# Attention's output projection by halves of the tokens, with the second tile's squares added on VectorE

## The chip, the cores and the metric

The kernel runs on one core of one Trainium2 chip. The metric is the device time of one execution in microseconds. Before the change it is 2884.4 us, the median of three runs (2883.95 to 2885.89).

## The reference

A trunk of two layers over 1040 tokens (1024 tokens with 16 meta tokens ahead of them), 1024 columns wide, all in float32. The first layer is a state-space mixer with a gated feed-forward network, the second a stick-breaking attention (16 heads of 64) with another such network. What the change touches is the end of the attention and the start of the last network:

```python
def _rmsnorm(x, g):
    x32 = x.astype(jnp.float32)
    y = x32 * lax.rsqrt(jnp.mean(x32 * x32, axis=-1, keepdims=True) + NORM_EPS)
    return (y * g.astype(jnp.float32)).astype(x.dtype)

def _conv_ffn(u, w_up, conv_w, conv_b, w_down):
    h = _causal_dwconv(u @ w_up, conv_w, conv_b)
    g, val = jnp.split(h, 2, axis=-1)
    return (jax.nn.silu(g) * val) @ w_down

    # in reference(), for each layer
            o = _stick_breaking_attention(q, k_shared, v_shared).reshape(b, L, SB_WIDTH)
            h = h + o @ sb_w_o[j]
        h = h + _conv_ffn(_rmsnorm(h, ffn_norm[layer]), ffn_w_up[layer], ffn_conv_w[layer],
                          ffn_conv_b[layer], ffn_w_down[layer])
    return _rmsnorm(h, final_norm)[:, N_META:]
```

The outputs of the meta tokens are dropped, so the second layer's network is computed for the 1024 others and for the two tokens ahead of them that its convolution needs.

## The kernel before

**Layout and precision.** The stream `h` is held with columns on partitions: eight rows of 128 columns, each a buffer with all tokens along it. The last stage works on four tiles of 256 tokens (the first 258 wide, with the two lead tokens), in two halves of two tiles. TensorE multiplies float32 as three products of rounded parts (`mm3`): high weight by high operand (L195), high by low (L196), low by high (L197). "A product" below is one such instruction. Before TensorE can use them, weights and operands are split:

- Weights go through `load_w`: SyncE issues the DMA (L176) into one of three buffers, ScalarE copies the high part (L182), and Pool subtracts it to make the low part (L99), in pieces of 256 columns. High and low parts have three buffers each.
- Halves of an attention row go through `split_half`: ScalarE copies (L213), VectorE subtracts (L214). Whole rows go through `split`, in thirds (L205, L206).
- Rows of `h`, operands and some weights share a pool of 28 row buffers.

**The output projection.** The attention leaves its result `o` in memory as eight pairs of heads, 128 columns each. `o_proj` first fetches and splits pairs 0 to 3 as whole rows and the first halves of pairs 4 and 5, while pairs 6 and 7 are still being computed by the attention. Then come the *blocks*: for each of the eight output rows one block of weights (`w_o_f[f]`, 768 columns for six pairs) and the four tiles, six pairs for the tiles of the first half and four for those of the second. Then `enter_ffn` runs the *tiles*: for each tile in turn all eight output rows with the pairs that were left, which are 6 and 7 for the tiles 0 and 1, and 4 to 7 for the tiles 2 and 3.

Each sum over pairs is collected in a PSUM bank, an *accumulator*, and VectorE adds it to `h` (`accumulate`, L520). The blocks take their banks from two pools with three banks together, the tiles from three pools with five.

**What follows each tile.** Its squares (ScalarE, `square_row`) are summed over partitions and rows on TensorE by a product with a matrix of ones: for tile 0 VectorE adds the eight rows' squares up first (L1045) and one such product follows (L1023); for the tiles 1 to 3 each row has its own (L1049). From the sums `factors` makes the norm's factors (ScalarE L975 to L977, VectorE L979 to L981). `forms` then makes what the up projection of a half multiplies: the normed rows (sixteen instructions on VectorE, L1071, called the products of the forms), differences of them (L1095), and high and low parts (ScalarE L1077, VectorE L1078). `store` writes the tile's rows of `h` to memory (L1010, in SyncE's queue). `up_weights` fetches and splits the up projection's weights (Pool, L99); `up` multiplies, and VectorE adds partial results in PSUM (L1217) before further products go on into the same bank.

**What sets the order.** The program is written engine by engine in the order of the code; around this place a scheduler places instructions of each engine by a simulated timeline, while the attention itself keeps the order that is written. Within an engine instructions run in that order, and SyncE issues the DMAs one by one.

## Time and profile before

| what | value |
| --- | --- |
| median of three runs | 2884.4 us |
| the profiled execution | 2880.28 us |
| its span | 2878.6 us |
| TensorE busy | 2826.2 us, 98% of the span |
| VectorE busy | 2093.7 us, 73% |
| ScalarE busy | 1630.2 us, 57% |
| Pool busy | 1626.2 us, 56% |
| granted TensorE clock, mean | 0.998 |

The span is the time from the first to the last recorded instruction; the execution's own time is 1.7 us longer. The profile names the engines PE (TensorE), PEld (its weight loads), DVE (VectorE), ACT (ScalarE), POOL and SP (SyncE). A row of a timeline gives the start from the beginning of the span, the duration, the engine, the line of the kernel, the instruction, its output and inputs and their shapes, and how many instructions it stands for; behind it, in brackets, how long the engine was idle before it and what ended that. The output projection and the four tiles lie between 2070 and 2190 us of the span; the last network follows to the end.

### The profile page before, as it was taken

To read this page: it belongs to the slowest core of one execution; us is meant where nothing else is said; L and a number is where in the kernel's file an instruction comes from. 1 tells how busy PE (TensorE), PEld (TensorE's weight loads), DVE (VectorE), ACT (ScalarE), POOL (GpSimd) and SP (SyncE) were. 2 spreads that over 40 slices of the span, in tenths; PEclk is the share of its full clock that TensorE was granted. 3 is DMA by queue.
4 is the path that set the end of the run, shared out by engine and by line. 5 is a ranking of instruction groups with operands and counts; after the bars stand their busy time and mean duration, and the time that the engine had idled before them with its cause. 6 is when DMAs were issued, how large, how long until landed. Compare 5 with 4: busy or idle time off the path is not lost.

```text
span 2878.6 us, 58687 instructions
## 1 busy us (share of the span) xinstructions
PE 2826.2 (98%) x21859; PEld 2710.5 (94%) x21859; DVE 2093.7 (73%) x4068; ACT 1630.2 (57%) x3393; POOL 1626.2 (56%) x2440
## 2 busy tenths in 40 slices
PE   8999999999999999999999999999999999999998
PEld 7989999999989999999999999999898999999888
DVE  5676666668597767676886888888759776767776
ACT  5554454543265656555336888887736555555433
POOL 2366455643529888868853222222363888886882
PEclk9999999999999999999999999999999999999999
DMA  4333334333412222244132222222432222225331
GB/s 118 85 112 98 114 86 135 105 131 101 130 59 97 77 80 78 79 167 159 53 121 71 65 61 70 61 59 54 138 115 75 80 80 81 76 82 183 110 103 67
DMA packets 135578, 274.51 MB, mean 95 GB/s; under 512 B 15827, under 2 KB 68188, under 8 KB 135292
## 3 DMA queue, kind: packets, MB, share of 16 engines
q1 hardware_dynamic: 129484, 258.85, 28.8%
q0 software_dynamic: 2096, 6.77, 0.6%
q10 hardware_dynamic: 3712, 5.15, 0.5%
q8 instruction: 172, 2.82, 0.4%
q14 instruction: 114, 0.93, 0.1%
HBM read 204.63 MB, written 51.16 MB: 89 GB/s over the span
## 4 chain that ended last, share of the span: by engine, by line
PE 45%; DVE 2%; ACT 1%; POOL 1%; issue 1%; DMA 0%; ACTq 0%; DVEq 0%; SPq 0%; POOLq 0%
PE p L197 5%; PE p L195 5%; PE p L196 5%; PE acc L197 4%; PE acc L195 4%; PE acc L196 4%; PE pj L195 3%; PE pj L196 3%; PE pj L197 3%; PE po L1658 3%; PE lg L1617 3%; PE wT L1644 3%; POOL wl L99 1%; DVE h L1071 0%; ACT bt L1621 0%
## 5 line engine op out<-in xcount | busy, mean ns | idle before, releaser
L99 POOL TENSOR_TENSOR wl<-w,wh 128x256 fp32r<-128x256 f32 x768 | 685.7, 924 | 367.3 <-ACT wh L182 265.9
L195 PE MATMUL pj<-uh,wh 128*128 128x348 f32 (+2 forms) x1536 | 501.4, 327 | 3.9 <-DVE qs L1568 1.6
L196 PE MATMUL pj<-ul,wh 128*128 128x348 f32 (+2 forms) x1536 | 495.2, 322 | 0.1
L197 PE MATMUL pj<-uh,wl 128*128 128x348 f32 (+2 forms) x1536 | 492.1, 320 | 0.0
L195 PE MATMUL p<-bh,fh 128*128 128x262 f32 (+1 forms) x1408 | 400.6, 285 | 5.5 <-DVE p L1217 5.5
L197 PE MATMUL p<-bh,fl 128*128 128x262 f32 (+1 forms) x1408 | 400.7, 285 | 1.9 <-POOL fl L99 1.9
L196 PE MATMUL p<-bl,fh 128*128 128x262 f32 (+1 forms) x1408 | 397.8, 283 | 0.1
L99 POOL TENSOR_TENSOR fl<-x,fh 128x256 fp32r<-128x256 f32 x352 | 265.1, 786 | 191.6 <-ACT fh L1154 165.7
L195 PE MATMUL p<-bh,wh 128*128 128x262 f32 (+1 forms) x1040 | 295.0, 284 | 1.9 <-ACT ft L1214 1.9
L196 PE MATMUL p<-bl,wh 128*128 128x262 f32 (+1 forms) x1040 | 295.3, 284 | 1.4 <-DVE bl L1078 1.4
L195 PEld LDWEIGHTS pj<-uh,wh 128*128 128x128 f32 x1536 | 289.0, 188 | 7.5 <-issue 1.9
L197 PE MATMUL p<-bh,wl 128*128 128x262 f32 (+1 forms) x1040 | 294.2, 283 | 0.0
L196 PEld LDWEIGHTS pj<-ul,wh 128*128 128x128 f32 x1536 | 289.5, 188 | 1.5 <-DVE ul L306 0.4
L197 PEld LDWEIGHTS pj<-uh,wl 128*128 128x128 f32 x1536 | 289.0, 188 | 0.1
L325 DVE SCALAR_TENSOR_TENSOR c<-p,params,c 128x260 f32<-128x260 f32 (+1 forms) x528 | 248.5, 480 | 54.9 <-ACT c L322 48.4
L195 PEld LDWEIGHTS p<-bh,fh 128*128 128x128 f32 x1408 | 267.4, 190 | 6.3 <-DVE p L1217 5.9
L197 PEld LDWEIGHTS p<-bh,fl 128*128 128x128 f32 x1408 | 266.6, 189 | 2.9 <-POOL fl L99 2.5
L196 PEld LDWEIGHTS p<-bl,fh 128*128 128x128 f32 x1408 | 267.7, 190 | 0.5 <-DVE bl L1078 0.4
L1214 ACT ACTIVATE ft<-p 128x262 f32<-128x262 f32 (+1 forms) x352 | 133.1, 383 | 176.4 <-DVE p L1217 110.3
L197 PE MATMUL acc<-gh,wl 128*128 128x260 f32 (+1 forms) x672 | 213.9, 320 | 2.6 <-POOL wl L99 2.5
L196 PE MATMUL acc<-gl,wh 128*128 128x260 f32 (+1 forms) x672 | 214.1, 320 | 0.0
L195 PE MATMUL acc<-gh,wh 128*128 128x260 f32 (+1 forms) x672 | 211.0, 320 | 3.0 <-DVE h L1378 2.9
(344 smaller groups left out, 7918.3 us busy)
## 6 DMA issues: line engine op xcount, KB each, us to landing
w<-in_w_up SPq DMA_DIRECT2D x88, 512.0 KB
w<-in_w_down SPq DMA_DIRECT2D x44, 512.0 KB
w<-in_w_in SPq DMA_DIRECT2D x40, 512.0 KB
E<-ea_d SPq DMA_DIRECT2D x32, 464.0 KB
D<-acs_d SPq DMA_DIRECT2D x32, 420.5 KB
g<-c SPq DMA_DIRECT2D x88, 130.0 KB
g<-c SPq DMA_DIRECT2D x88, 128.0 KB
b<-g SPq DMA_DIRECT2D x16, 520.0 KB
```

The source lines that it names most:

```text
L99: eng.tensor_tensor(out[:, c], x[:, c], y[:, c], op=op)
L195: self.behind(mm(out, wh, uh, start=first, stop=False, skip_group_check=joins), tie, "behind the sums of squares")
L196: mm(out, wh, ul, start=False, stop=False, skip_group_check=joins)
L197: self.last_mm = mm(out, wl, uh, start=False, stop=last, skip_group_check=joins)
L325: ins = nc.vector.scalar_tensor_tensor(out, ps[:, o + i : o + i + n], wcol(i), out, op0=ALU.mult, op1=ALU.add)
L1214: nc.scalar.activation(s[:, :N], ps[:, :N], AF.Copy)
L1617: nc.tensor.matmul(ps[:nt, :m], part[:, c0 : c0 + nt], ks[a][:, s0 : s0 + m], start=x == 0, stop=x == 1)
L1644: nc.tensor.transpose(pt[:ns, x * CB : x * CB + nt], bt[a][:nt, x * CB : x * CB + ns], self.ident[:nt, :nt])
L1658: nc.tensor.matmul(po[64 * a : 64 * a + 64, :nt], v[: CH[c][1], c, 64 * a : 64 * a + 64], wt[a][: CH[c][1], c, :nt], start=x == 0, stop=x ...
```

## The change

In the second layer the work is put in another order, by halves of the tokens:

- **Blocks by halves.** First the eight rows' blocks for the tiles 0 and 1 (six pairs), then the tiles 0 and 1 with pairs 6 and 7, then the eight rows' blocks for the tiles 2 and 3 (pairs 0 to 3), then the tiles 2 and 3 with pairs 6, 7, 4 and 5. Each block's weights are fetched and split once for each half (768 columns, then 512 of them again).
- **Operands.** Every row of `o` is fetched and split as a half; the second half's operands are made behind the tiles of the first.
- **Forms.** The factors of tile 1 and the forms of the first half run beside the blocks of the second half; before, they ran beside the tiles 2 and 3.
- **Squares.** Tile 1's squares are added on VectorE, as tile 0's were, and one product with ones follows in place of eight.
- **Up weights.** The first block of up weights is split behind the blocks of the second half; before, ahead of the tiles.

The first layer calls the same function with a pair in place of the callable, and keeps its order.

```diff
--- before.py
+++ after.py
@@ -957,12 +957,12 @@
         def operands(x):
             made[x] = last[x][0], last[x][1]()
 
-        def tile(j, work):
+        def tile(j, work, m=1):
             ws, ops = made[j // 2]
             ms[j] = self.sm("ms")
             for f in range(KD):
                 self.accumulate(h, f, *g.span(j), lambda i, f: (ws[i][0][:, f * P : f * P + P], ws[i][1][:, f * P : f * P + P]), ops, HB, next(banks), g.part(j // 2)[0])
-                self.square_row(ms[j], h, f, *g.span(j), KD if j == 0 else 1)
+                self.square_row(ms[j], h, f, *g.span(j), m)
                 next(work, None)
 
         def factors(j):
@@ -1010,24 +1010,31 @@
                 nc.sync.dma_start(d[k, :, c : c + n], h[k][:, HB + c : HB + c + n])
 
         self.after_factors = None
-        ws0 = list(self.up_weights(layer, 0, pool))[-1]
+        split = callable(last[1])
+        if not split:
+            ws0 = list(self.up_weights(layer, 0, pool))[-1]
         operands(0)
-        tile(0, iter(()))
+        tile(0, iter(()), KD)
         store(0)
-        operands(1)
+        if not split:
+            operands(1)
         forms = [form_tiles()]
         work = self.forms(layer, h, r, 0, forms[0], pool)
 
-        def first(sums):
+        def first(j, sums, n):
             yield
-            nc.tensor.matmul(ms[0][:, : g.span(0)[1]], self.ones, sums, start=True, stop=True)
-            factors(0)
+            nc.tensor.matmul(ms[j][:, : g.span(j)[1]], self.ones, sums, start=True, stop=True)
+            factors(j)
             yield
-            yield from islice(work, 3)
-
-        tile(1, first(self.squares))
-        factors(1)
+            yield from islice(work, n)
+
+        tile(1, first(0, self.squares, 3), KD if split else 1)
         store(1)
+        if split:
+            made[1] = last[1](first(1, self.squares, KD))
+            ws0 = list(self.up_weights(layer, 0, pool))[-1]
+        else:
+            factors(1)
         for j in (2, 3):
             tile(j, work)
             factors(j)
@@ -1742,18 +1749,27 @@
             self.nc.sync.dma_start(t, od[p, :, g.at + s0 : g.at + s0 + m])
             return self.split_half(t, "o")
 
-        tiles = [(n // 3 * i, n // 3) for i in range(3)]
-        ops = [self.split(fetch(od[p], "o"), "o", tiles=tiles) for p in range(first - 2)]
-        ops = [ops + [part(p, 0) for p in (first - 2, first - 1)], ops]
-        for f in range(KD):
-            w = self.load_w(a["w_o_f"][f], first * P)
-            h[f] = fetch(hd[f], "h")
-            for j in range(4):
-                self.accumulate(h, f, *g.span(j), lambda i, f: (w[0][:, i * P : i * P + P], w[1][:, i * P : i * P + P]), ops[j // 2], HB, base=-g.lead)
+        def columns(x, count, ops, work):
+            for f in range(KD):
+                w = self.load_w(a["w_o_f"][f, :, : count * P], count * P)
+                if x == 0:
+                    h[f] = fetch(hd[f], "h")
+                for j in (2 * x, 2 * x + 1):
+                    self.accumulate(h, f, *g.span(j), lambda i, f: (w[0][:, i * P : i * P + P], w[1][:, i * P : i * P + P]), ops, HB, base=g.part(x)[0])
+                next(work, None)
+
+        columns(0, first, [part(p, 0) for p in range(first)], iter(()))
         ops = [part(p, 0) for p in range(first, PAIRS)]
-        ws = [self.load_wd(a["w_o"][first - 2 + i], i < 2) for i in range(4)]
-        second = [part(p, 1) for p in range(first - 2, PAIRS)]
-        return self.enter_ffn(1, h, [(ws[2:], lambda: ops), (ws, lambda: second)], pool)
+        ws = [self.load_wd(a["w_o"][p], True) for p in range(first, PAIRS)]
+        other = [part(p, 1) for p in range(first - 2)]
+
+        def between(work):
+            order = *range(first, PAIRS), *range(first - 2, first)
+            rest = [part(p, 1) for p in order]
+            columns(1, first - 2, other, work)
+            return ws + [self.load_wd(a["w_o"][p], False) for p in order[2:]], rest
+
+        return self.enter_ffn(1, h, [(ws, lambda: ops), between], pool)
 
 
     def finish(self, h, j):
```

**On VectorE, behind tile 1.** Below is VectorE's order before, from one addition of an accumulator of tile 2 to the next. `h` are rows of the stream, `acc` accumulators, `r` the row of the norm's factors, `y` and `yy` steps on the way to it, `params` the norm's gains.

```order
L520 TENSOR_TENSOR h_27110<-h_27110,acc_28020 128x256
L980 TENSOR_TENSOR y_27875<-y_27875,yy_27880 128x258
L981 SCALAR_TENSOR_TENSOR r_27714<-y_27875,r_27714 128x258
L1071 SCALAR_TENSOR_TENSOR h_27032<-h_27032,params,r_27714 128x258
L1071 SCALAR_TENSOR_TENSOR h_27110<-h_27110,params,r_27714 128x258
L1071 SCALAR_TENSOR_TENSOR h_27188<-h_27188,params,r_27714 128x258
L1071 SCALAR_TENSOR_TENSOR h_27266<-h_27266,params,r_27714 128x258
L1071 SCALAR_TENSOR_TENSOR h_27344<-h_27344,params,r_27714 128x258
L1071 SCALAR_TENSOR_TENSOR h_27422<-h_27422,params,r_27714 128x258
L1071 SCALAR_TENSOR_TENSOR h_27500<-h_27500,params,r_27714 128x258
L1071 SCALAR_TENSOR_TENSOR h_27578<-h_27578,params,r_27714 128x258
L520 TENSOR_TENSOR h_27188<-h_27188,acc_28041 128x256
```

The eight products of the forms stand between two additions of tile 2; `acc_28020` and `acc_28041` are two of the tiles' accumulators, which have five banks. VectorE's order of the changed kernel, around the same products:

```order
L1052 TENSOR_TENSOR sq_27559<-sq_27559,sq_27630 128x256
L520 TENSOR_TENSOR h_27012<-h_27012,acc_27715 128x256
L1078 SCALAR_TENSOR_TENSOR h_27012<-h_27012,params,r_27452 128x258
L1078 SCALAR_TENSOR_TENSOR h_27062<-h_27062,params,r_27452 128x258
L1078 SCALAR_TENSOR_TENSOR h_27112<-h_27112,params,r_27452 128x258
L1078 SCALAR_TENSOR_TENSOR h_27162<-h_27162,params,r_27452 128x258
L1078 SCALAR_TENSOR_TENSOR h_27212<-h_27212,params,r_27452 128x258
L1078 SCALAR_TENSOR_TENSOR h_27262<-h_27262,params,r_27452 128x258
L1078 SCALAR_TENSOR_TENSOR h_27312<-h_27312,params,r_27452 128x258
L1078 SCALAR_TENSOR_TENSOR h_27362<-h_27362,params,r_27452 128x258
L1052 TENSOR_TENSOR sq_27559<-sq_27559,sq_27655 128x256
L520 TENSOR_TENSOR h_27012<-h_27012,acc_27729 128x256
```

Here they stand between two additions of the second half's blocks (`acc_27715` is the first accumulator of row 0, `acc_27729` its second), with additions of tile 1's squares (`sq`) around them: the addition that frees one of the blocks' three banks is queued behind all eight.

**On SyncE, where the tiles' weights and operands are fetched.** Before, behind the last two blocks: `w` are weight buffers, `o` halves of attention rows, `in_w_o` the weights of the tiles' pairs, `in_w_up` the up weights, `hm` the stored stream.

```order
L176 DMA w_4080_27570<-in_w_o_f 128x768
L176 DMA w_4094_27660<-in_w_o 128x1024
L176 DMA w_4097_27669<-in_w_o 128x1024
L1742 DMA o_27694<-o_d 128x512
L176 DMA w_4098_27676<-in_w_o 128x1024
L1742 DMA o_27699<-o_d 128x512
L176 DMA w_4101_27685<-in_w_o 128x1024
L1742 DMA o_27704<-o_d 128x512
L1147 DMA w_4113_27716<-in_w_up 128x1024
L1742 DMA o_27709<-o_d 128x512
L1148 DMA w_4114_27717<-in_w_up 128x1024
L1010 DMA hm_27715<-h_27110 128x256
```

All of these stand ahead of the first store of a tile. In the changed kernel, at the end of the second half's blocks:

```order
L1010 DMA hm_27453<-h_27362 128x256
L176 DMA w_4179_27961<-in_w_o_f 128x512
L1749 DMA o_27688<-o_d 128x512
L176 DMA w_4186_28006<-in_w_o_f 128x512
L1749 DMA o_27693<-o_d 128x512
L1749 DMA o_27698<-o_d 128x512
L176 DMA w_4191_28049<-in_w_o 128x1024
L1749 DMA o_27703<-o_d 128x512
L176 DMA w_4194_28058<-in_w_o 128x1024
L1154 DMA w_4197_28067<-in_w_up 128x1024
L1155 DMA w_4198_28068<-in_w_up 128x1024
```

The operand halves of the last tiles, the last two rows of output weights and the first up weights now stand behind the stores of tiles 0 and 1 and among the fetches of the second half's block weights (`in_w_o_f`, 512 columns).

## The prediction

> **What bounds the kernel now.** I read the page first, then the busy time by stretches around the change, then the timelines of TensorE (PE), VectorE (DVE), Pool and SyncE there.
>
> ```profile
> span 2878.6 us, 58687 instructions
> PE 2826.2 (98%) x21859; PEld 2710.5 (94%) x21859; DVE 2093.7 (73%) x4068; ACT 1630.2 (57%) x3393; POOL 1626.2 (56%) x2440
> ...
> core 0: us, PE busy (x) PEld busy (x) DVE busy (x) ACT busy (x) POOL busy (x), PEclk, DMA share, GB/s
> 2070.70:2078.70 8.00, 7.91 (x58) 6.92 (x54) 6.05 (x15) 4.84 (x12) 0.00 (x0) 1.00 0.62 232
> 2078.70:2143.50 64.80, 64.78 (x536) 64.76 (x536) 27.29 (x60) 20.58 (x30) 36.90 (x50) 1.00 0.42 135
> 2143.50:2173.00 29.50, 29.13 (x217) 28.00 (x215) 27.44 (x68) 18.01 (x51) 9.60 (x16) 1.00 0.17 61
> 2173.00:2190.40 17.40, 12.97 (x89) 11.39 (x88) 17.30 (x49) 8.15 (x21) 0.00 (x0) 1.00 0.20 76
> ```
>
> TensorE is the bound of the kernel as a whole. The four stages here are its start on the output projection, the projection's blocks with the first two tiles (no idle time to speak of), tiles 2 and 3, and the step into the up projection. In the last two VectorE is the full engine, 44.7 us busy of 46.9, and TensorE waits for it at the end:
>
> ```profile
> PE p L195 <- DVE p L1217: 3.6, 1, 3.6
> ...
> 2070.74 0.51 PE L195 MATMUL acc<-oh,wh 128*128 128x258 f32 x2
> ...
> 2078.74 0.39 PE L195 MATMUL acc<-oh,wh 128*128 128x256 f32 x1
> ...
> 2143.56 0.59 PE L1049 MATMUL ms<-sq,ones 128*128 128x256 f32 x2
> ...
> 2148.53 0.59 PE L1049 MATMUL ms<-sq,ones 128*128 128x256 f32 x2
> 2148.77 0.47 PE L197 MATMUL acc<-o,wl 128*128 128x256 f32 x1
> 2149.08 0.59 PE L1049 MATMUL ms<-sq,ones 128*128 128x256 f32 x2
> ...
> 2186.45 0.28 PE L197 MATMUL p<-bh,wl 128*128 128x258 f32 x1
> 2190.37 0.54 PE L195 MATMUL p<-bh,fh 128*128 128x258 f32 x1 [3.63 <-DVE p L1217]
> 2190.71 0.42 PE L196 MATMUL p<-bl,fh 128*128 128x258 f32 x1
> 2190.93 0.42 PE L197 MATMUL p<-bh,fl 128*128 128x258 f32 x1
> ```
>
> The order has 535 products from the start at 2078.74 to the first sum of squares at 2143.56, so one product takes 64.82 / 535 = 0.121 us of TensorE's time. From 2148.53 to 2149.08 lie one sum of squares (two instructions in the trace, one row in the order) and one product: the sum costs 0.55 - 0.12 = 0.43 us.
>
> Everything that the change moves lies between two points that both programs share: A, the first product of the projection (2070.74), and B, the up projection's product that waits for an addition (2190.37). A to B is 119.63 us: 840 products (101.6), 25 sums of squares (10.8), and 7.3 us of waiting. Of that 1.5 us is at the start (54 products in 8.00 us instead of 6.5) and 5.8 us is after the tiles, the 3.6 us gap among it. This 7.3 is nearly all there is to win; the order of the engines outside A to B is the same in both programs.
>
> **The change, part by part.**
>
> *Seven sums of squares leave TensorE.* Tile 1's eight become one: 7 x 0.43 = 3.0 us less, on the engine that is the bound. VectorE gets seven additions in their place.
>
> *The start.* Before, four rows are split in thirds, twelve pieces, and two more as halves; now six halves are. On the path stand ScalarE's copy and VectorE's subtraction.
>
> ```profile
> 2074.98 1.14 ACT L213 ACTIVATE o<-o 128x514 fp32r<-128x514 f32 x2
> ...
> 2075.91 1.29 DVE L214 TENSOR_TENSOR o<-o,o 128x514 fp32r<-128x514 f32 x2
> ```
>
> VectorE makes a half in 0.65 us. The first is ready when A comes, the second about 1.8 us later (ScalarE has the last attention copy between), the others every 0.65 to 1.0 us; each feeds nine products, 1.1 us. So TensorE loses about 0.7 us instead of 1.5.
>
> *The blocks of the second half.* This is where the change can lose. Before, all blocks run ahead of the tiles, and VectorE has little beside them (27.3 us of 64.8). Now 192 products of the second half's blocks (23.2 us) run behind tile 1, and the first half's forms run beside them. A block's accumulators use three PSUM banks, so TensorE cannot go on more than about two accumulators (2.9 us) ahead of VectorE's additions, and these stand in VectorE's queue between the forms. The order puts 70 instructions of VectorE between the last addition of tile 1 and that of the 15th block accumulator, itself the 71st. TensorE has 234 products and one sum of squares from the start of tile 1's last accumulator to the product that waits for that bank: 28.3 + 0.4 = 28.7 us. VectorE's durations:
>
> ```profile
> 2140.37 0.41 DVE L520 TENSOR_TENSOR h<-h,acc 128x256 f32<-128x256 f32 x1
> 2140.70 0.63 DVE L1045 TENSOR_TENSOR sq<-sq,sq 128x258 f32<-128x258 f32 x1
> 2141.25 0.74 DVE L520 TENSOR_TENSOR h<-h,acc 128x256 f32<-128x256 f32 x2
> ...
> 2146.11 0.97 DVE L979 TENSOR_TENSOR yy<-r 128x258 f32<-128x258 f32 x1
> ...
> 2148.89 5.55 DVE L1071 SCALAR_TENSOR_TENSOR h<-h,params,r 128x258 f32<-128x258 f32 x8
> ...
> 2158.72 0.42 DVE L980 TENSOR_TENSOR y<-y,yy 128x256 f32<-128x256 f32 x1
> ...
> 2159.84 3.25 DVE L1071 SCALAR_TENSOR_TENSOR h<-h,params,r 128x256 f32<-128x256 f32 x8
> 2163.01 1.43 DVE L1095 TENSOR_TENSOR ft<-h 128x258 f32<-128x258 f32 x4
> ...
> 2140.11 5.98 POOL L99 TENSOR_TENSOR fl<-x,fh 128x256 fp32r<-128x256 f32 x8
> ...
> 2149.40 1.79 POOL L99 TENSOR_TENSOR x<-x,w 128x256 f32<-128x256 f32 x2
> 2151.24 1.71 POOL L99 TENSOR_TENSOR x<-w,x 128x256 f32<-128x256 f32 x2
> ...
> 2202.03 5.41 POOL L99 TENSOR_TENSOR fl<-x,fh 128x256 fp32r<-128x256 f32 x4 [29.63 <-ACT fh L1154]
> ```
>
> With Pool idle (2159.84) the eight products of the forms take 0.405 us each, start to start; beside Pool they took 5.55 us together. Pool stopped at 2152.95: if the ones behind it ran at 0.405, the first five intervals were about 0.85 each. An addition of squares beside Pool takes 0.55 (2140.70 to 2141.25); without it I take 0.335, as for the subtractions (four in 1.43). With Pool idle the 71 sum to: 15 additions from PSUM x 0.335 (2141.25) = 5.0, 6 of squares 2.0, 6 for two tiles' factors x 0.42 (2158.72) = 2.5, 16 products 6.5, 24 low parts and subtractions 8.0, 4 operand halves 2.6: **26.6 us**. With Pool always busy: 5.0 + 6 x 0.55 + 6 x 0.97 (2146.11) + 16 x 0.85 + 24 x 0.55 + 4 x 0.65 x 0.55 / 0.335 = **45.2 us**; the rates for the low parts and the halves are estimates from the addition's. VectorE begins about 1.6 us late (it adds tile 1's last accumulator when that is done). Excess over TensorE: 26.6 + 1.6 - 28.7 = -0.5 us at one end, 18.1 us at the other.
>
> Pool is what the change brings here: five blocks' weights (two pieces each) and one row of output weights (four) are split in this stretch, 14 pieces; before, Pool was through at 2152.95, ahead of the second set of products. A piece takes 0.75 us (2140.11), 0.87 (2151.24) or 1.35 (2202.03) with VectorE dense: 10.5 to 18.9 us of some 35.5, a share of 0.30 to 0.53. Between the two ends that gives 5.1 to 9.4 us; I take the middle, 7.2. Against the low end: the second eight products come just when the last block's weights and the output weights are split, and TensorE cannot take its next bank before they are through.
>
> The Trainium skill, SBUF — State Buffer, section SBUF: two separate sides, says that the port pair which VectorE and GpSimd share is "an exclusive lock, not a bandwidth split", also for VectorE instructions with two SBUF inputs: the later one blocks. By that rule each piece holds up one instruction, by up to 0.85 - 0.405 us; 14 pieces would be 6.2 us, the excess 5.7, and the result 1.5 us better than mine. The products' two rates above agree with it.
>
> *Operand halves of the second half.* The second of the last four is fetched in SyncE's queue behind the last block's weights, which wait for a buffer that Pool frees.
>
> ```profile
> 2113.36 0.33 SPq L1742 DMA_DIRECT2D o<-o_d  x1
> ...
> 2117.17 0.63 ACT L213 ACTIVATE o<-o 128x512 fp32r<-128x512 f32 x1 [3.18 <-DMA o<-o_d]
> ```
>
> A half takes 3.8 us from issue to ScalarE's copy (2113.36 to 2117.17). VectorE's queue holds its subtraction ahead of two block additions, so it can idle 0 to 3.8 us there; most of it overlaps with waiting for TensorE, and I take 0.5. Loss in the middle: 7.2 + 0.5 = **7.7 us**.
>
> *The end.* Behind the last product of tile 3 TensorE has 72 products and two sums up to B: 9.6 us. VectorE must add the accumulator that TensorE finishes 24 products and two sums on (3.8 us, with its latency 4.0), then do the same 18 instructions as before.
>
> ```profile
> 2182.77 0.43 DVE L1217 TENSOR_TENSOR p<-p,ft 128x258 f32<-128x258 f32 x1
> ...
> 2189.89 0.42 DVE L1217 TENSOR_TENSOR p<-p,ft 128x258 f32<-128x258 f32 x1
> ```
>
> From the first addition to B it took 2190.37 - 2182.77 = 7.6 us: B comes at 4.2 + 7.6 = 11.8, a wait of 2.2 us where 5.8 were lost. This needs VectorE to have no backlog, and it has 39 instructions beside the 25 us of tiles 2 and 3. Bounds: 0, and 5.8 if the backlog stays.
>
> *Clock.* Behind the 3.63 us gap products take 0.215 instead of 0.121 us (2190.37, next at 2190.71 and on) for some 15 products, 1.4 us, in a stretch where VectorE is full anyway; I put its going at 0, and its coming in the middle at 0 to 1.4.
>
> *Hidden.* Weights are loaded in twice as many pieces: 8 x 256 KB more DMAs, copies on ScalarE (57% busy) and 2 Pool pieces a block. A block now lasts 24 products, 2.9 us, against 2 x 0.75 to 2 x 1.35 us of Pool and less on ScalarE, with three buffers. The first up weights are split after that: 22 pieces, 16 to 30 us, begun some 35 us behind tile 1's last accumulator (the end of the blocks) and needed at about 62 (389 products, 16 sums, 7.7 of loss): covered by 11 us, or short by 3 if each piece took 1.35.
>
> **Sum**, against the profiled execution: A to B = 101.6 + 18 x 0.43 (7.7) + 0.7 + 7.7 + 2.2 = 119.9 us, before 119.63: 0.3 us more. That execution took 2880.28 us in all (span 2878.6), 0.14% under the median of 2884.4; with the same difference the median is **2884.7 us**.
>
> **The rivals.** *A: VectorE keeps pace* (0.17). If Pool's pieces fall beside instructions that don't suffer, the middle loses only bank waits, about 1.5 us, and the end as above: 7.3 - 0.7 - 1.5 - 2.2 + 3.0 = 5.9 us gained; with no wait at the end 8.1, so 2876.3. For it: VectorE's own 26.6 us fit in 28.5, and between 2078.7 and 2143.5 it was idle 58%. Against: the first set of products alone (3.2 us, with the addition behind it) is longer than the lead of the banks.
>
> *B: VectorE behind Pool all through* (0.20). If VectorE and Pool hold each other up for the whole stretch, the middle costs 18.1 + 0.5 us: 119.9 - 7.7 + 18.6 = 130.8, 11.2 us slower, 2895.6. The sign turns at a Pool share of 0.40; 0.2% is passed at 0.71 (an excess of 12.7), or at 0.52 if the backlog reaches the end (5.8 for 2.2). For it: the two rates of the products; against: Pool has 14 pieces.
>
> *C: weights late* (0.05). If the fetches behind the 16 stores of tiles 0 and 1 in SyncE's queue come late, TensorE waits for a block's weights: 0.2% would take 5.8 us, two blocks' whole length. For it: SyncE issues in order; against: the stores wait only for additions that TensorE needs too. Late up weights are part of it, 3 us by the bound above.
>
> **How the numbers follow.** My forecast of no change has 0.58; about 0.2% (5.8 us) is what a measurement of this kernel tells from none. The range 2878 to 2891: below, the middle at 2.5 with the end at 0.5 (6.9 us less); above, the middle at 12, the clock's 1.4 and 0.6 more at the end (6.3 us more). It leaves out the far ends of A and B. Faster 0.17 (A), slower 0.25 (B and C), within 0.58.
>
> **What would show it.** Right: TensorE's seven sums gone; several waits of 0.5 to 3 us for additions (L520) behind tile 1 where there was none; products there at over 0.5 us beside Pool; the gap at B near 2 us. Wrong: no idle TensorE in the second half's blocks (A); over 12 us of it (B); waits for weight pieces on Pool or a DMA (C); or B's gap unchanged.

## The result, and the profile after

The changed kernel takes 2891.88 us in the median (2891.03 to 2893.79, eight runs). Against the kernel before on the same chips (2881.78 us in the median of eight runs) the ratio is 1.0031, with a 95% interval of 1.0022 to 1.0041: 8.9 us slower (6.3 to 11.8). I had forecast 2884.7 us, 0.3 us slower, in a range that reached 6.6 us above the time before (2891 us). The slowdown lies above that, and the median itself 0.9 us above the range.

The head of its page, and its busy time by stretches between the prediction's points A (the first product of the output projection) and B (the up projection's product that waits for an addition):

```profile
span 2889.5 us, 58733 instructions
PE 2829.3 (98%) x21845; PEld 2713.9 (94%) x21845; DVE 2106.7 (73%) x4071; ACT 1637.1 (57%) x3397; POOL 1638.1 (57%) x2456
...
core 0: us, PE busy (x) PEld busy (x) DVE busy (x) ACT busy (x) POOL busy (x), PEclk, DMA share, GB/s
2073.16:2119.60 46.44, 46.40 (x380) 46.19 (x379) 22.62 (x49) 18.89 (x33) 22.23 (x29) 0.99 0.58 191
2119.60:2138.30 18.70, 16.22 (x126) 15.32 (x125) 17.53 (x39) 9.74 (x24) 6.59 (x8) 1.00 0.39 124
2138.30:2164.30 26.00, 21.94 (x161) 20.86 (x160) 23.68 (x44) 13.46 (x29) 17.75 (x21) 0.93 0.23 75
2164.30:2201.03 36.73, 30.70 (x218) 29.04 (x216) 28.75 (x61) 13.65 (x35) 17.68 (x24) 0.95 0.24 87
sum 127.87, PE 115.26 PEld 111.42 DVE 92.59 ACT 55.74 POOL 64.24; mean PE 28.81 PEld 27.85 DVE 23.15 ACT 13.94 POOL 16.06
```

A to B takes 127.87 us where it took 119.63, 8.2 us more, and that is where the change's cost lies. The stretches are the first half's blocks and tiles up to tile 0's sum, then up to tile 1's sum, then up to tile 2's first sum, then tiles 2 and 3 and the step to B. VectorE was busy 78.0 us between the points and is now busy 92.6, for seven additions more; Pool went from 46.5 to 64.2. TensorE's waits, in its timeline:

```profile
2130.19 0.39 PE L195 MATMUL acc<-o,wh 128*128 128x256 f32 x1 [1.99 <-DVE h L520]
2149.42 0.43 PE L195 MATMUL acc<-o,wh 128*128 128x256 f32 x1 [2.35 <-DVE h L520]
2158.53 0.39 PE L195 MATMUL acc<-o,w 128*128 128x256 f32 x1 [0.90 <-DVE h L520]
2170.61 0.58 PE L195 MATMUL acc<-o,w 128*128 128x256 f32 x1 [3.52 <-DVE h L520]
2191.27 0.70 PE L1056 MATMUL ms<-sq,ones 128*128 128x256 f32 x2 [0.67 <-ACT sq L1050]
2201.03 0.39 PE L195 MATMUL p<-bh,fh 128*128 128x258 f32 x1 [1.84 <-DVE p L1224]
```

Four waits are for additions of accumulators (L520) that VectorE makes late; the wait at B has shrunk from 3.63 to 1.84 us. Why VectorE is late is read from its timeline, and from Pool's at the same time:

```profile
2120.99 0.42 DVE L520 TENSOR_TENSOR h<-h,acc 128x256 f32<-128x256 f32 x1 [0.73 <-PE acc L197]
...
2124.23 4.72 DVE L1078 SCALAR_TENSOR_TENSOR h<-h,params,r 128x258 f32<-128x258 f32 x8
...
2129.73 0.41 DVE L520 TENSOR_TENSOR h<-h,acc 128x256 f32<-128x256 f32 x1
...
2142.92 6.12 DVE L1078 SCALAR_TENSOR_TENSOR h<-h,params,r 128x256 f32<-128x256 f32 x8
2148.95 0.41 DVE L520 TENSOR_TENSOR h<-h,acc 128x256 f32<-128x256 f32 x1
...
2154.54 3.60 DVE L1102 TENSOR_TENSOR ft<-h,h 128x258 f32<-128x258 f32 x4
2158.06 0.41 DVE L520 TENSOR_TENSOR h<-h,acc 128x256 f32<-128x256 f32 x1
...
2167.55 2.68 DVE L1085 TENSOR_TENSOR bl<-ft,bh 128x258 fp32r<-128x258 f32 x3
2170.15 0.41 DVE L520 TENSOR_TENSOR h<-h,acc 128x256 f32<-128x256 f32 x1
```

```profile
2125.98 1.80 POOL L99 TENSOR_TENSOR wl<-w,wh 128x256 fp32r<-128x256 f32 x2 [13.40 <-ACT wh L182]
...
2143.13 5.23 POOL L99 TENSOR_TENSOR wl<-w,wh 128x256 fp32r<-128x256 f32 x6 [3.15 <-ACT wh L182]
2153.21 3.77 POOL L99 TENSOR_TENSOR wl<-w,wh 128x256 fp32r<-128x256 f32 x4 [4.85 <-ACT wh L182]
2156.94 1.79 POOL L99 TENSOR_TENSOR x<-w 128x256 f32<-128x256 f32 x2
...
2164.67 3.54 POOL L99 TENSOR_TENSOR wl<-w,wh 128x256 fp32r<-128x256 f32 x4
...
2169.04 3.52 POOL L99 TENSOR_TENSOR fl<-x,fh 128x256 fp32r<-128x256 f32 x4
```

The first row is the addition of tile 1's last accumulator. The eight products of the first set (2124.23) take 4.72 us, beside two of Pool's pieces and part of two more; those of the second set take 6.12 us beside six, where beside an idle Pool they took 3.25 before. Each late addition comes behind such a run (at 2129.73 with one addition of squares between), and TensorE's product just behind the addition. What is new against the prediction is that this goes on in tile 2: from 2156.94, behind pieces of the output weights, Pool splits the first up weights, and low parts (L1085) and differences (L1102) take about 0.9 us apiece. The groups of VectorE say the same for the low parts, first of before (2143.5 to 2190.4 us), then of after (2138 to 2172 us):

```profile
L1078 DVE TENSOR_TENSOR bl<-ft,bh 128x258 fp32r<-128x258 f32 x16 | 6.0, 417 | 0.0
```

```profile
L1085 DVE TENSOR_TENSOR bl<-ft,bh 128x258 fp32r<-128x258 f32 x12 | 9.9, 874 | 0.0
```

### The profile page after: what moved, and what is told of

It is laid out like the page before. It is cut to its first block, busy times and chain, and to the rows that moved or that the text cites. A ratio compares the mean times of both kernels' runs of the same rounds, so it can differ in the third digit from the quotient of the medians.

```text
span 2889.5 us, 58733 instructions
## 1 busy us (share of the span) xinstructions
PE 2829.3 (98%) x21845; PEld 2713.9 (94%) x21845; DVE 2106.7 (73%) x4071; ACT 1637.1 (57%) x3397; POOL 1638.1 (57%) x2456
## 4 chain that ended last, share of the span: by engine, by line
PE 43%; DVE 3%; ACT 1%; POOL 1%; issue 1%; DMA 1%; DVEq 0%; SPq 0%; ACTq 0%; POOLq 0%
PE p L196 5%; PE p L197 5%; PE p L195 5%; PE acc L195 4%; PE acc L197 4%; PE acc L196 4%; PE pj L195 3%; PE pj L196 3%; PE pj L197 3%; PE po L1665 3%; PE lg L1624 3%; PE wT L1651 3%; POOL wl L99 1%; DVE bl L1085 1%; DVE h L1078 1%
## 5 line engine op out<-in xcount | busy, mean ns | idle before, releaser
L99 POOL TENSOR_TENSOR wl<-w,wh 128x256 fp32r<-128x256 f32 x784 | 699.4, 922 | 379.6 <-ACT wh L182 274.2
```

Of the source, the lines that this page charges most:

```text
L99: eng.tensor_tensor(out[:, c], x[:, c], y[:, c], op=op)
```

## The experiments

Executions of one kernel scatter, by 2.8 us among the eight of the changed kernel and by 11 us among the eleven of sq_back. In the two traces of before, whose spans differ by 3.8 us, A to B differs by 0.1; so the parts are compared by the time from A to B in one traced execution each, and the ratio of whole times stands beside it. The last column says how far that execution lay from the median of its kernel. Those of sq_back and halves_once were the fastest of their eleven: their time from A to B may be shorter than that of a usual execution, and their whole times count for more. Those of no_low_banks5 and blocks_first reach A at 2077.57 and 2076.47 us, where the others have it at 2070.7 to 2074.5, so that part of their excess lies ahead of A.

| kernel | A to B, us | VectorE busy | Pool busy | ratio to before (95%) | traced execution less median, us |
| --- | --- | --- | --- | --- | --- |
| before | 119.63 | 78.0 | 46.5 | | -1.5 |
| changed | 127.87 | 92.6 | 64.2 | 1.0031 (1.0022 to 1.0041) | -0.7 |
| sq_alone | 124.74 | 81.4 | 47.5 | 1.0023 (1.0014 to 1.0033) | +0.9 |
| sq_back | 120.97 | 83.5 | 63.7 | 1.0016 (1.0007 to 1.0025) | -6.3 |
| banks5 | 126.63 | 94.4 | 63.5 | 1.0022 (1.0013 to 1.0031) | -0.1 |
| late_forms | 126.96 | 87.5 | 62.0 | 1.0019 (1.0010 to 1.0028) | +1.2 |
| no_up_low | 122.09 | 82.9 | 44.4 | 1.0006 (0.9997 to 1.0015) | -0.3 |
| no_both_low | 120.04 | 80.2 | 32.0 | 1.0002 (0.9993 to 1.0011) | +0.7 |
| no_low_banks5 | 115.10 | 80.8 | 31.3 | 0.9991 (0.9982 to 1.0000) | +4.1 |
| sq_back_banks5 | 125.73 | 88.1 | 63.1 | 1.0020 (1.0011 to 1.0030) | +2.0 |
| blocks_first | 126.14 | 83.9 | 61.4 | 1.0018 (1.0009 to 1.0027) | +4.2 |
| halves_once | 118.55 | 77.9 | 46.3 | 1.0010 (1.0001 to 1.0019) | -2.9 |

**Are the two points steady?** Both kernels as they are, once more.

> The changed kernel once more, for a second trace. If the 127.9 us between the two points belong to the kernel, they come again within 1 us. If a good part is the phase of TensorE's clock behind waits (slow products at the first product of the projection and behind gaps), they differ by 1 to 3 us.

> The kernel before once more, for a second trace. If the 119.6 us between the two points belong to the kernel, they come again within 1 us. If its trace was a fortunate one (its execution was 1 to 3 us under the median of the runs), 120.5 to 122.5.

The stretch from A to B of the two new traces:

```profile
2072.78:2201.15 128.37, 116.40 (x879) 112.72 (x877) 92.00 (x192) 55.45 (x120) 63.76 (x81) 0.96 0.38 127
```

```profile
2073.20:2192.73 119.53, 114.72 (x893) 111.32 (x891) 77.24 (x187) 51.53 (x114) 46.88 (x65) 1.00 0.34 115
```

They come again within 0.5 us (128.37 after 127.87) and 0.1 us (119.53 after 119.63): the difference belongs to the kernels. The point A itself is not steady: it came 2.4 us later in the first trace of the changed kernel than in the first of before, and 2.5 us later in the second trace of before too. That part is not the change's; the last section returns to it.

**The squares alone.** The kernel before, with tile 1's squares added on VectorE.

```diff
-                self.square_row(ms[j], h, f, *g.span(j), KD if j == 0 else 1)
+                self.square_row(ms[j], h, f, *g.span(j), KD if j <= layer else 1)
...
         tile(1, first(self.squares))
+        if layer:
+            nc.tensor.matmul(ms[1][:, : g.span(1)[1]], self.ones, self.squares, start=True, stop=True)
         factors(1)
```

> The kernel before with one part of the change: tile 1's squares are added on VectorE and summed by one product with ones. Theory 'TensorE': the seven sums cost TensorE 0.43 us each, so 3.0 us less than before. Rival 'VectorE sets the end': up to the product that waits for the up projection's first addition VectorE is the full engine (44.7 of 46.9 us busy), seven more additions cost it 7 x 0.34 to 7 x 0.55 = 2.4 to 3.9 us, and the wait at the end grows by as much as TensorE saves: within 1 us of before.

```profile
2074.23:2198.97 124.74, 112.75 (x878) 110.09 (x876) 81.39 (x194) 50.68 (x114) 47.48 (x65) 0.97 0.33 110
```

5.1 us slower between the points, worse than either theory. VectorE's timeline shows why:

```profile
2153.62 5.18 DVE L1073 SCALAR_TENSOR_TENSOR h<-h,params,r 128x258 f32<-128x258 f32 x8
...
2164.41 0.41 DVE L1047 TENSOR_TENSOR sq<-sq,sq 128x256 f32<-128x256 f32 x1
...
2169.13 0.42 DVE L979 TENSOR_TENSOR yy<-r 128x256 f32<-128x256 f32 x1
...
2171.01 3.26 DVE L1073 SCALAR_TENSOR_TENSOR h<-h,params,r 128x256 f32<-128x256 f32 x8
```

The additions of squares (L1047) stand in one queue with the first half's products and low parts. The last is made at 2164.41, tile 1's sum follows on TensorE at 2167.22, its factors come at 2169.13, and the second set of products begins 96.8 us behind A (2171.01 less 2074.23) where it began 89.1 us behind A before (2159.84 less 2070.74): 7.7 us later, on the engine that sets B. Summed on TensorE, the squares had no such queue to wait in. TensorE's new waits are 3.44 us for a tile's addition behind the first set of products (ended at 2159.51) and 3.25 us for a low part in the step to B (2192.64); the one at B is 3.60 (before: 3.63).

**The squares put back.** The changed kernel with tile 1's squares on TensorE.

```diff
-        tile(1, first(0, self.squares, 3), KD if split else 1)
+        tile(1, first(0, self.squares, 3), 1)
...
+            if j == 0:
                 nc.tensor.matmul(ms[j][:, : g.span(j)[1]], self.ones, sums, start=True, stop=True)
```

> The changed kernel with tile 1's squares summed row by row on TensorE again. If TensorE sets the pace there, 3.0 us slower than the changed kernel. If VectorE does, its seven additions (0.34 to 0.95 us each beside Pool) go and TensorE's waits shrink by about as much as the sums cost: within 1.5 us of the changed kernel.

```profile
2072.36:2193.33 120.97, 114.45 (x893) 111.98 (x891) 83.46 (x185) 55.98 (x120) 63.65 (x81) 0.98 0.41 135
```

6.9 us less than the changed kernel, though TensorE has 3.0 us more to do. Both theories missed it. The size is less sure than the sign, since this execution lies 6.3 us under the kernel's median: by the whole times (1.0016 against 1.0031) the gain is about 4 us. Tile 1's factors come 11.4 us earlier: VectorE's first step of them stands at 57.0 us behind A (2129.38) where the changed kernel has it at 68.4 (2141.54):

```profile
2129.38 0.74 DVE L979 TENSOR_TENSOR yy<-r 128x256 f32<-128x256 f32 x1
```

```profile
2141.54 0.43 DVE L979 TENSOR_TENSOR yy<-r 128x256 f32<-128x256 f32 x1
```

The forms then end 0.9 us behind tile 2's first sum (2162.49 and 2161.60), where in the changed kernel they go on for 8.5 us behind it, and the wait of 3.52 us there is gone. Not all of this need be the squares' queue: Pool's first piece comes 3.9 us later behind A than in the changed kernel, so the first set of products runs beside an idle Pool, in 3.27 us in place of 4.72. What is left, 1.3 us above before in this trace and 4.6 by the whole times (2.0 to 7.2), is the reordering itself.

**Five banks.** The second half's blocks take accumulators from all five banks.

```diff
+        banks = cycle((self.mm, self.lg, self.ex, self.mm, self.lg))
...
-                    self.accumulate(h, f, *g.span(j), lambda i, f: (w[0][:, i * P : i * P + P], w[1][:, i * P : i * P + P]), ops, HB, base=g.part(x)[0])
+                    self.accumulate(h, f, *g.span(j), lambda i, f: (w[0][:, i * P : i * P + P], w[1][:, i * P : i * P + P]), ops, HB, next(banks) if x else None, base=g.part(x)[0])
```

> The changed kernel with the second half's blocks taking their accumulators from all five banks in place of three. Theory 'lead': TensorE stops because it may run only two accumulators ahead of additions that stand behind the forms; with four it is 2.9 us further ahead, the gaps of 1.99, 2.35 and 0.90 us for block additions go, with the slow products behind them: 5 to 7 us faster than the changed kernel. Rival 'backlog': VectorE has too much to do beside Pool over the whole stretch; the waits only move to tile 2, whose accumulators have five banks already (3.52 us there now): at most 2 us faster.

```profile
2071.22:2197.85 126.63, 114.12 (x879) 111.43 (x877) 94.43 (x192) 56.01 (x120) 63.52 (x81) 0.96 0.39 129
```

```profile
2161.64 0.58 PE L195 MATMUL acc<-o,w 128*128 128x256 f32 x1 [5.28 <-DVE h L520]
```

1.2 us less, as the rival "backlog" said. Waits that were spread come together in one of 5.28 us.

**Pool's splitting left out.** The first up weights' pieces alone, then these and the second half's block weights. High parts stand in for the low parts, sums and differences that are left out; the number of products stays.

```diff
+        if b == 0 and layer == 1:
...
+            for t, n, p, tag in ((g, D, self.wp, "wh"), (v, D, pool, "fh"), (g, D, pool, "fh"), (v, H, self.wp, "w32")):
+                hi = p.tile([P, 1024], F32R, tag=tag, name=self.nm(tag))
+                nc.scalar.activation(hi[:, :n], t[:, D - n : D], AF.Copy)
+                his.append((hi, hi))
...
-        pieces(nc.gpsimd, wl[:, :n], w32[:, :n], wh[:, :n].bitcast(F32), ALU.subtract)
+        if not low:
+            return wh, wh
+        pieces(nc.gpsimd, wl[:, :n], w32[:, :n], wh[:, :n].bitcast(F32), ALU.subtract)
```

> The changed kernel without Pool's 22 pieces for the first up weights only (high parts in their place). If these are what my sum missed (I had them start behind the blocks, and they start some 20 us behind tile 1 and run beside the forms and tile 2): the 3.52 us wait in tile 2 with the slow products behind it goes, and part of the waits ahead of it, 4 to 8 us less than the changed kernel between the two points (120 to 124 us in place of 127.9). If the block weights' pieces are the main part: less than 2 us.

> The changed kernel without Pool's subtractions for the second half's block weights (16 pieces) and for the first up weights (22 pieces): the high parts stand in for the low ones and for the sums and differences of the up weights. TensorE, VectorE and the weights' copies on ScalarE have the work of the changed kernel (four copies of the up weights as there). Theory 'Pool': VectorE runs at its rates beside an idle Pool, the stretch needs 26.6 us against TensorE's 28.7, and the 10 us lost in the second half's blocks, the 5 in tile 2 and the wait at the end shrink to 1 to 4 together: from the first product of the projection to the up projection's product that waits for an addition 111 to 115 us in place of 127.9. Rival 'work': the forms and additions are too much for VectorE there in any case: over 120 us.

```profile
2073.26:2195.35 122.09, 114.67 (x879) 112.08 (x877) 82.91 (x192) 55.31 (x120) 44.38 (x59) 0.95 0.41 134
```

```profile
2073.69:2193.73 120.04, 112.32 (x879) 109.78 (x877) 80.20 (x192) 54.96 (x120) 32.01 (x43) 0.98 0.41 136
```

The 22 pieces of the up weights were worth 5.8 us, inside what I expected of them, and the block weights' 16 pieces another 2.1. Without the first, the waits of 0.90 and 3.52 us are gone; those of 1.99 and 2.36 us ahead of them stay. In the changed kernel these pieces begin 35.5 us behind tile 1's last addition (2156.94 less 2121.41), as the prediction had it, and not 20 as the first of the two texts above has it. VectorE has the same 192 instructions in all three kernels and is busy 92.6, 82.9 and 80.2 us: Pool is what makes the difference. But 120.0 is not the 111 to 115 of the theory "Pool". Nor was Pool idle, as that theory and the next expectation have it: eight pieces of the output weights are still split beside the forms, and the second set of products meets the first four of them.

```profile
2142.06 5.16 DVE L1080 SCALAR_TENSOR_TENSOR h<-h,params,r 128x256 f32<-128x256 f32 x8
```

```profile
2143.06 3.49 POOL L99 TENSOR_TENSOR wl<-w,wh 128x256 fp32r<-128x256 f32 x4 [34.33 <-ACT wh L182]
```

It takes 5.16 us, and TensorE's wait of 2.03 us stands behind it (ended at 2147.95). So this kernel alone does not say what would be left with Pool idle.

**Both: Pool's splitting left out, and five banks.**

> The changed kernel without Pool's subtractions for the second half's block weights and the first up weights (120.0 us between the two points when that was done alone), and with five banks for the second half's blocks. What was left with Pool idle were waits of 2.03, 0.64 and 2.02 us for additions behind the forms, with slow products behind them. Theory 'bursts': VectorE has the time, but its eight products and other forms stand in a row ahead of the addition that frees a bank; with two more banks these waits go: 113 to 116 us. Rival 'work': VectorE is behind over the whole stretch even so, the waits move to tile 2 as with Pool working (1.2 us gained there by the banks): 118 to 121 us.

```profile
2077.57:2192.67 115.10, 110.72 (x878) 108.60 (x876) 80.76 (x192) 55.09 (x120) 31.25 (x43) 0.99 0.41 142
```

Without the 38 pieces the two banks are worth 4.9 us, with them 1.2. So bursts are the other part. The first set of products, beside an idle Pool, takes 3.27 us and made TensorE wait 0.44 with three banks and not at all with five; the second, beside pieces of the output weights, takes 6.32 us here and makes it wait 1.19. More lead covers such runs if VectorE catches up in between, and beside all of Pool's pieces it did not. What the bursts alone would cost, with no piece of Pool's beside them, no run here shows.

**The forms beside tiles 2 and 3 again.**

```diff
-            made[1] = last[1](first(1, self.squares, KD))
+            made[1] = last[1](iter(()))
+            late = first(1, self.squares, 16)
...
-            tile(j, work)
+            tile(j, late if split else work)
...
```

> The changed kernel with tile 1's factors and the first half's forms run beside tiles 2 and 3, as before the change, in place of beside the second half's blocks. All theories: the 10 us that TensorE loses in the second half's blocks shrink to about 1.5. Theory 'Pool': the first up weights' 22 pieces on Pool now lie beside all the forms and hold VectorE up by some 0.4 us each, about 8 us, so the wait for the up projection's first addition grows from 5.8 (before) to about 14: some 5 us slower than before the change. Rival 'lead' (Pool is not what costs): the wait there is 5.8 as before the change, and the whole is 2 to 3 us faster than before.

```profile
2073.36:2200.32 126.96, 116.20 (x879) 112.58 (x877) 87.49 (x192) 55.84 (x120) 62.01 (x81) 0.95 0.39 129
```

```profile
2171.93 1.22 PE L1057 MATMUL ms<-sq,ones 128*128 128x256 f32 x2 [3.23 <-ACT sq L1051]
...
2200.32 0.39 PE L195 MATMUL p<-bh,fh 128*128 128x258 f32 x1 [3.56 <-DVE p L1225]
```

Slower than before by 7.3 us between the points, which excludes the rival; but the wait at B is 3.56 us and not 14. The time is lost on the way: VectorE's queue stands beside the up weights' pieces, TensorE waits 3.23 us for a row's squares behind it, and its clock is at 0.95 (before: 1.00).

**Blocks of both halves ahead of the tiles.** Squares and forms as before; what differs from before is the halves of the attention rows and the weights loaded and split twice.

```diff
         columns(0, first, [part(p, 0) for p in range(first)], iter(()))
+        other = [part(p, 1) for p in range(first - 2)]
+        columns(1, first - 2, other, iter(()))
...
```

> The kernel before with the blocks by halves (halves of the attention rows, weights of the second half's blocks loaded again), both halves' blocks ahead of the tiles, tile 1's squares on TensorE and the forms beside tiles 2 and 3 as before. If loading and splitting the weights twice costs nothing (Pool has 28 us idle there and gets 12 to 14 us more): 0.8 us less than before, from the start alone, 118.8 us between the two points. Rival: Pool's extra pieces push its splitting of the output and up weights beside the forms, and VectorE, which sets the end, is held up: 2 to 6 us more than before.

```profile
2076.47:2202.61 126.14, 117.45 (x892) 113.65 (x891) 83.89 (x185) 55.15 (x120) 61.44 (x81) 0.96 0.39 129
```

```profile
2155.80 7.02 DVE L1078 SCALAR_TENSOR_TENSOR h<-h,params,r 128x258 f32<-128x258 f32 x8
```

```profile
2156.33 7.10 POOL L99 TENSOR_TENSOR fl<-x,fh 128x256 fp32r<-128x256 f32 x8
```

6.5 us slower than before between the points, just above the rival's 2 to 6. The extra pieces push Pool's work on the up weights back to where the forms begin: eight products take 7.02 us beside eight pieces, and TensorE then waits 3.76 us for a row's squares (ended at 2171.33). Here Pool is through some 94 us behind A; before it was 82 (2152.95 less 2070.74), when the forms had hardly begun.

**Halves alone.** The kernel before, pairs 0 to 3 fetched and split as halves, weights once.

```diff
-        tiles = [(n // 3 * i, n // 3) for i in range(3)]
-        ops = [self.split(fetch(od[p], "o"), "o", tiles=tiles) for p in range(first - 2)]
-        ops = [ops + [part(p, 0) for p in (first - 2, first - 1)], ops]
+        ops = [[part(p, 0) for p in range(first)], [part(p, 1) for p in range(first - 2)]]
...
```

> The kernel before with one part of the change: pairs 0 to 3 are fetched and split as halves in place of whole rows in thirds; blocks, weights, tiles, squares and forms as before. By the prediction the start costs TensorE 0.7 us in place of 1.5: 54 products in about 7.2 us in place of 8.0, 118.8 us between the two points in place of 119.6, and a time within 0.1% of before. Rival: the start is set by the last pairs of the attention and the clock there, and nothing changes or it gets worse by a phase of the clock (up to 2 us).

```profile
2071.99:2190.54 118.55, 113.48 (x892) 110.21 (x890) 77.86 (x185) 51.81 (x112) 46.34 (x65) 1.00 0.37 129
```

1.1 us less between the points, near the 0.8 expected, and at the start itself 54 products take 7.14 us in place of 8.00. The whole is no faster for it but 0.1% slower (1.0010): behind B TensorE waits for the up weights' parts,

```profile
2201.98 0.58 PE L195 MATMUL p<-bh,fh 128*128 128x258 f32 x1 [1.24 <-ACT fh L1154]
...
2205.05 0.58 PE L197 MATMUL p<-bh,fl 128*128 128x258 f32 x1 [1.84 <-POOL fl L99]
```

3.1 us, where the first trace of before shows one wait of 0.96. Whether the rest of the 0.1% is of the same kind stays open.

**Squares back and five banks.** The two edits shown above together, as a version that might beat before.

> The changed kernel with tile 1's squares summed row by row on TensorE again (121.0 us between the two points when that was done alone) and five banks for the second half's blocks. Theory 'lead': without the squares VectorE's backlog is small enough for two more banks to cover it: the waits of 2.37 and 1.17 us go with the slow products behind them, 116 to 118 us, and some 2 us faster than before the change. Rival 'backlog': the wait moves to tile 2: 120 to 122 us.

```profile
2074.50:2200.23 125.73, 117.11 (x893) 113.73 (x891) 88.14 (x185) 55.72 (x120) 63.06 (x81) 0.97 0.39 130
```

It does not. Between the points it is 4.8 us worse than the squares put back alone, but the trace of those lies 6.3 us under its median; by the whole times the two can't be told apart (1.0020 and 1.0016). VectorE is busy 88.1 us for the same 185 instructions that took 83.5: more of them may have fallen beside Pool's pieces. The scheduler also put them in another order, and which of the two came first is not settled. None of the variants that compute the whole is faster than the kernel before.

## Why the prediction held in part and failed in part

**Seven sums leave TensorE: the step that failed most.** I booked 3.0 us of gain and put the seven additions into VectorE's load. The load was about right (sq_alone: VectorE 3.4 us more busy). What I left out was the wait: tile 1's sum, and with it the factors and the second set of products, must now come through VectorE's queue behind the first set. Alone it made the kernel 5.1 us slower between the points (6.6 by the whole times, where I had 3.0 us faster); taking it out of the changed kernel gained 6.9 in one trace and about 4 by the whole times. How close the change without its squares comes to my 0.3 us stays open: 1.3 us in that trace, 4.6 by the whole times. This loss is no term beside those that follow; it shows up in the middle and at the end.

**The start, 0.7 us: right.** A to tile 0's sum is 378 products, 45.7 us, and took 46.44. The same step done alone took 0.9 us off the start and 1.1 off A to B.

**The blocks of the second half, 7.7 us: right in kind, 2.4 too small.** The stretches up to tile 2's first sum hold 279 products and two sums, 34.6 us, and took 44.7 (2119.6 to 2164.3): 10.1 us lost. The 71 instructions took 37.1 us, from the end of tile 1's last addition at 2121.4 to 2158.5, between my ends of 26.6 and 45.2. Pool did about 19 pieces in it in place of 14 and was busy half of the time, within my 0.30 to 0.53; I had taken the middle. The wait for an operand half on VectorE was 2.3 us, inside 0 to 3.8.

**The end, 2.2 us: failed.** Tiles 2 and 3 up to B hold 183 products and 16 sums, 29.0 us, and took 36.73: 7.7 us lost, above even the 5.8 that I gave as the bound. The wait at B is 1.84 us, as forecast; the rest lies in tile 2, where I had none. The step said that VectorE would have no backlog, and I had costed the up weights' 22 pieces only by whether TensorE would wait for them. It doesn't. But they run beside VectorE just when it has to catch up: without them A to B shrinks by 5.8 us. The middle's 2.4 and the 5.5 here are nearly all that I missed between the points (127.9 against 119.9). (The sum of this step counts 4.2 us where the sentence ahead of it has 4.0, a slip of 0.2.)

**The rivals.** A fell. B's price of 11.2 us was nearer to the result than my forecast, and it came about by the condition named there: a share of Pool near 0.52 (0.50 in the stretch) and a backlog that reaches the end. It is not B in full, since VectorE did not stand behind Pool all through. C fell: of the waits for weights, those on Pool's low parts are 0.5 us at most.

**The rule on the shared port.** The second set's eight products took 6.12 us beside six pieces and 3.25 alone: 0.48 us for each piece, close to the 0.85 - 0.405 that I had read as one instruction held up. The Trainium skill, SBUF — State Buffer, section SBUF: two separate sides, has it so (the later of the two blocks), and this trace agrees with it, as do eight products and eight pieces side by side in 7.02 and 7.10 us in blocks_first; no run here tells a lock from a shared rate. The sum by that rule was 1.5 us under mine, and the middle came out above both: the rate was right, the count of pieces too low. With 19 pieces the same sum gives, as an estimate, 8.0 us, and with the 2.3 us wait for the operand half 10.3, against the 10.1 measured.

**The clock.** I allowed 0 to 1.4 us, and it was 2.8. Behind the wait that ended at 2149.42, products ran at 0.21 us each until 2153.05 (granted clock 0.53), 17 of them, 1.6 us more than at 0.121; behind the one at 2170.61 about ten more (0.50), 1.2 us. Both are inside the losses above.

## What to carry to other kernels

When a sum is moved from a full engine to one with idle time, ask not only whether that engine has the time but what stands ahead in its queue and who waits for the sum: here 3.0 us saved on TensorE left the kernel 4 to 7 us slower, since the sum had to come through VectorE's queue. And when weights are split again, or split later, look at what VectorE does at that moment, even where TensorE never waits for a weight: in the kernel before Pool was nearly through when the forms began, and blocks_first, where its work came beside them, was 6.5 us slower between the points. More buffers help an engine that is late in bursts, not one that is behind throughout (4.9 us against 1.2 here).

## What had not been expected of the hardware

The clock behind waits depends on more than the length of the wait. At the end of the attention TensorE waits 0.7 to 1.0 us before each of the last two or three groups of transposes, in all fourteen traces. The 36 products behind them, first in one trace of before, then in the other:

```profile
2068.86 1.95 PE L1658 MATMUL po<-wt,v 116*64 116x112 f32 x36
```

```profile
2069.64 3.63 PE L1658 MATMUL po<-wt,v 116*64 116x112 f32 x36
```

The same instructions of the same program took 1.95 us at a granted clock of 1.00 and 3.63 us at 0.50, most of the 2.5 us by which A moved. The waits ahead were not quite the same: two in the first trace (0.69 and 1.03 us), three in the second (0.98, 1.03 and 0.73). So it is in all traces: 1.95 us behind two waits (before and banks5), 2.92 to 3.63 behind three. Behind the wait of 1.99 us that ended at 2130.19 in the changed kernel hardly a product is slow (granted clock 1.00); behind that of 2.35 us, with two of 0.28 and 0.48 ahead of it, 17 are, for 3.6 us. So the price of a wait is not set by its length alone, and this is one reason why single times of these kernels scatter by some microseconds.

The Trainium skill, TensorE: Matmul & The Clock Gate, section What's actually happening, gives a cause: the clock goes to half behind a window of about 3.4 us in which TensorE was idle, and the windows run freely, not from the kernel's start. The granted clock of 0.50 to 0.53 (0.21 us a product in place of 0.121), the length of 3.6 us and the change from one execution to the next agree with it; that waits of 0.7 to 1.0 us with 0.47 to 0.78 us of work between them are enough, as at the end of the attention, goes further than that rule. Where the windows lay in an execution, no run here shows.
